# Nearest-neighbour upsampling on one core: rows owned in two blocks of 261 and 251 a partition, with new load and store sizes

## The chip, the core and the metric

The kernel runs on one core of one Trainium2 chip. The metric is the device time of one execution in microseconds, as the median of several executions. Besides the matrix engine, which does nothing here, the core has VectorE (DVE in the profile), ScalarE (ACT), GpSimd (POOL) and SyncE (SP). SP issues the DMA transfers of this kernel. The transfers are carried by 16 DMA engines that move data between HBM and the on-chip memory, which has 128 partitions.

## The reference: what is computed

The input `x` is a float32 array of 16 x 64 x 64 x 64 (batch, channel, row, column), 16.78 MB. Every pixel is repeated twice in each direction, which gives 16 x 64 x 128 x 128, or 67.11 MB:

```python
for i in range(new_h):
    for j in range(new_w):
        result[:, :, i, j] = x[:, :, i // scale_factor, j // scale_factor]
```

There is no arithmetic. The kernel reads every byte of the input once, copies it four times within the on-chip memory, and writes the copies.

## The kernel before, in words

All input rows of all images are numbered in one list of 65,536 rows of 64 floats (256 bytes). Partition p owns R = 512 rows that follow each other in memory: rows 512p to 512p + 511. One input row becomes two output rows of 128 floats, 1,024 bytes in all, which also follow each other in HBM, so that partition p's output is one piece of 512 KB. "A row" below always means an input row: 256 bytes to load, 1 KB a partition to store.

One on-chip tile, `mem`, holds everything. Its upper part, the view `xt`, takes the whole input (512 rows a partition). Below it are `FREE` = 79 rows' worth of output space, 79 KB a partition. Three loads bring in 8 rows, 248 rows and 256 rows a partition (`HEAD`, `cuts`, line 151). They are taken out of the kernel's body by `begin_before_barrier` and issued by SP as its first instructions.

The output is made in nine groups of 62, 32, 48, 64, 50, 64, 64, 64 and 64 rows (the list `rows`). For each group VectorE copies the rows into a buffer, with every element twice and every row twice (line 170, `expanded`); the first group takes two copies of 31 rows. Then SP stores the buffer with one transfer (line 171). There is one packet for each partition in each transfer, so each of the 16 DMA engines has eight packets of every transfer and works through its transfers in the order in which SP issues them.

Groups with an even number use the bottom of `mem`. Those with an odd number use a place that moves up: it ends where the input rows not yet expanded begin, and overwrites rows that have been expanded already. So a copy must wait until an earlier store has read its buffer: group 2 waits for store 0, group 3 for store 1, group 4 for store 2, and so on, always two groups back. Store n waits for copy n. Counting from 0, then, while store n - 1 moves, copy n has to run, so that store n is in the queue when store n - 1 ends. Group 4 is the one with 50 rows before the change.

`close_early` rewrites the end of the program so that the clearing of semaphores lies beside the last store; SP's last instruction waits for that store alone.

Of the kernel before, what the change touches and what calls it, by code (L numbers as in the profile page):

```python
# [1 line left out]

# [4 lines left out]

EARLY = 3  # L10


def begin_before_barrier(nc):

    blocks = nc.main_func.blocks
    main, body = blocks[0], blocks[1]
    sp = mybir.EngineType.SP
    loads = [i for i in body.instructions if i.engine == sp][:EARLY]  # L20
    for load in loads:
        assert isinstance(load, mybir.InstDMACopy), type(load)
        assert not (load.sync_info and load.sync_info.on_wait)
    names = [i.name for i in loads]
    body.instructions = [i for i in body.instructions if i.name not in names]
    kept = list(main.instructions)
    at = next(
        n
        for n, i in enumerate(kept)
        if i.engine == sp and isinstance(i, mybir.InstDrain)  # L30
    )
    kept[at:at] = loads
    main.instructions = kept


def close_early(nc):

    blocks = nc.main_func.blocks  # L40
    sp, pool = mybir.EngineType.SP, mybir.EngineType.Pool
    stores = [
        i
        for i in blocks[1].instructions
        if i.engine == sp and isinstance(i, mybir.InstDMACopy)
    ]
    last = stores[-1].sync_info.on_update[0].id

    end = list(blocks[-1].instructions)
    wait = end[0]  # L50
    assert wait.engine == sp and isinstance(wait, mybir.InstDrain)
    waits = list(wait.sync_info.on_wait)
    assert len({w.id for w in waits}) == len(waits) > 2
    assert all(w.wait_mode == "sem-ge-imm" for w in waits)

    mine = [i for i in end if i.engine == pool]
    kinds = [type(i).__name__ for i in mine]
    assert kinds == [
        "InstDrain",
        "InstEventSemaphore",  # L60
        "InstEventSemaphore",
        "InstDrain",
        "InstISA",
        "InstDrain",
        "InstEventSemaphore",
        "InstEventSemaphore",
    ], kinds
    d0, gather0, release0, d1, clear, d2, gather1, release1 = mine


    lo, hi = clear.ant_dict["range_first"], clear.ant_dict["range_last"]
    assert lo <= last <= hi and all(lo <= w.id <= hi for w in waits)
    clears = []
    for a, b in ((lo, last), (last + 1, hi + 1)):
        if a < b:
            clears.append(nc.gpsimd.sem_clear(range(a, b)).ins)

    landed = mybir.InstDrain(
        name=wait.name,
        engine=pool,  # L80
        debug=wait.debug,
        sync_info=mybir.SyncInfo(
            on_wait=[w for w in waits if w.id != last], on_update=[]
        ),
    )
    (w,) = [w for w in waits if w.id == last]
    final = mybir.InstEventSemaphore(
        name=clear.name,
        engine=sp,
        debug=wait.debug,  # L90
        sync_info=mybir.SyncInfo(
            on_wait=[w],
            on_update=[
                mybir.SyncUpdate(
                    sync_type=w.sync_type,
                    id=w.id,
                    ant_name=w.ant_name,
                    update_mode="sem-sub-imm",
                    update_value=w.wait_value,
                )  # L100
            ],
        ),
    )
    others = [i for i in end if i.engine != pool and i is not wait]
    blocks[-1].instructions = others + [
        d0, gather0, release0, gather1, release1, d1, landed, *clears, d2, final
    ]


@with_exitstack  # L110
def kernel(
    ctx: ExitStack,
    tc: tile.TileContext,
    x: bass.AP,
    scale_factor: int,
    out: bass.AP,
):
    nc = tc.nc
    nc.at_finalize(begin_before_barrier)
    nc.at_finalize(close_early)  # L120
    P = nc.NUM_PARTITIONS
    s = int(scale_factor)
    B, C, H, W = x.shape
    R = B * C * H // P
    fdt = x.dtype

    xp = x.rearrange("b c h w -> (b c h) w").rearrange("(p r) w -> p r w", p=P)
    op = out.rearrange("b c (h hd) w -> (b c h) (hd w)", hd=s).rearrange(  # L130
        "(p r) w -> p r w", p=P
    )

    rows = [62, 32, 48, 64, 50, 64, 64, 64, 64]
    GROW = s * s
    FREE = 79
    WF = FREE * GROW * W  # L140
    assert sum(rows) == R
    mem_pool = ctx.enter_context(tc.tile_pool(name="mem", bufs=1))
    mem = mem_pool.tile([P, WF + R * W], fdt, name="mem")
    xt = mem[:, WF:].rearrange("p (r w) -> p r w", r=R)

    HEAD = 8
    cuts = [0, HEAD, R // 2, R]
    for lo, hi in zip(cuts, cuts[1:]):  # L150
        nc.sync.dma_start(out=xt[:, lo:hi], in_=xp[:, lo:hi])  # L151

    def expanded(r0, r1):
        return (
            xt[:, r0:r1].unsqueeze(2).unsqueeze(4).to_broadcast([P, r1 - r0, s, W, s])
        )

    r0 = 0
    before = (0, 0)
    for n, k in enumerate(rows):  # L160
        size = k * GROW * W
        at = 0 if n % 2 == 0 else WF + r0 * W - size
        assert at >= before[1] or at + size <= before[0]
        before = (at, at + size)
        u = mem[:, at : at + size].rearrange(
            "p (k a w b) -> p k a w b", k=k, a=s, w=W
        )
        parts = [0, 31, k] if n == 0 else [0, k]
        for a, b in zip(parts, parts[1:]):
            nc.vector.tensor_copy(out=u[:, a:b], in_=expanded(r0 + a, r0 + b))  # L170
        nc.sync.dma_start(out=op[:, r0 : r0 + k, :], in_=u)
        r0 += k


# [1 line left out]
_INS = ['x', 'scale_factor']  # L176
_OUTS = [((16, 64, 128, 128), 'float32')]

_NUMBERS = {'scale_factor': 2}


# [26 lines left out]
```

## Time and profile before

| What | Value |
|---|---|
| Time, median of 3 runs (lowest to highest) | 197.09 us (197.07 to 197.12) |
| The profiled execution: its own time | 197.16 us |
| Its span, first to last instruction | 195.8 us |
| What lies around the span | 1.36 us |
| VectorE busy | 78.0 us (40% of the span), 10 copies |
| DMA packets, bytes | 1728, 83.89 MB |
| Share of the 16 DMA engines' span taken by packets | 99.2% |
| Mean rate over the span | 428 GB/s |

The profile gives the busy time of each engine, the busy share of the DMA engines in 40 slices, groups of instructions by form, and the chain of work that ended last. The trace behind it holds a start and a duration for every DMA packet too. An element of a shape is one float; "128x12800" is 128 partitions with 50 rows of 256 floats. A wait is named for what ended it: `DVE mem <- DMA out_dram<-mem` is VectorE waiting for a store.

### The profile page before, as it was taken

To read this page: it belongs to the slowest core of one execution; us is meant where nothing else is said; L and a number is where in the kernel's file an instruction comes from. 1 tells how busy PE (TensorE), PEld (TensorE's weight loads), DVE (VectorE), ACT (ScalarE), POOL (GpSimd) and SP (SyncE) were. 2 spreads that over 40 slices of the span, in tenths; PEclk is the share of its full clock that TensorE was granted. 3 is DMA by queue.
4 is the path that set the end of the run, shared out by engine and by line. 5 is a ranking of instruction groups with operands and counts; after the bars stand their busy time and mean duration, and the time that the engine had idled before them with its cause. 6 is when DMAs were issued, how large, how long until landed. Compare 5 with 4: busy or idle time off the path is not lost.

```text
span 195.8 us, 76 instructions
## 1 busy us (share of the span) xinstructions
DVE 78.0 (40%) x10; POOL 0.2 (0%) x4
## 2 busy tenths in 40 slices
DVE  0000599980007579085008907900890088000000
POOL 0000000000000000000000000000000000000000
DMA  9999999999999999899987989999999999999994
GB/s 456 415 428 415 428 428 428 428 415 415 415 415 428 428 482 482 375 469 495 469 384 345 502 348 455 442 469 482 469 442 428 428 428 442 428 428 428 428 428 214
DMA packets 1728, 83.89 MB, mean 428 GB/s; under 512 B 192, under 2 KB 192, under 8 KB 320
## 3 DMA queue, kind: packets, MB, share of 16 engines
q1 hardware_dynamic: 1728, 83.89, 99.2%
HBM read 16.78 MB, written 67.11 MB: 428 GB/s over the span
## 4 chain that ended last, share of the span: by engine, by line
DMA 60%; DVE 24%; SPq 0%; issue 0%; DVEq 0%
DMA out_dram<-mem 49%; DVE mem L170 24%; DMA mem<-in_x_dram 11%; SPq L151 0%; DVEq L170 0%
## 5 line engine op out<-in xcount | busy, mean ns | idle before, releaser
L170 DVE COPY mem<-mem 128x16384 f32<-128x16384 f32 (+4 forms) x10 | 78.0, 7812 | 87.8 <-DMA out_dram<-mem 65.8
L189 POOL MEMSET const-uint8-127<- 128x1 uint8 x1 | 0.1, 102 | 0.0
L189 POOL MEMSET const-bfloat16-1.0<- 128x1 bf16 x1 | 0.1, 101 | 0.0
L189 POOL MEMSET const-float32-0.0<- 128x1 f32 x1 | 0.1, 98 | 0.2 <-issue 0.2
L189 POOL MEMSET const-float32-1.0<- 128x1 f32 x1 | 0.1, 98 | 0.0
## 6 DMA issues: line engine op xcount, KB each, us to landing
mem<-in_x_dram SPq DMA_DIRECT2D x1, 7936.0 KB, 21.5
out_dram<-mem SPq DMA_DIRECT2D x1, 7936.0 KB, 21.2
out_dram<-mem SPq DMA_DIRECT2D x1, 6400.0 KB, 27.6
out_dram<-mem SPq DMA_DIRECT2D x1, 6144.0 KB, 17.5
out_dram<-mem SPq DMA_DIRECT2D x1, 4096.0 KB, 26.4
mem<-in_x_dram SPq DMA_DIRECT2D x1, 256.0 KB, 2.7
out_dram<-mem SPq DMA_DIRECT2D x5, 29.8
mem<-in_x_dram SPq DMA_DIRECT2D x1, 40.4
```

The costliest lines, as they stand in the source:

```text
L170: nc.vector.tensor_copy(out=u[:, a:b], in_=expanded(r0 + a, r0 + b))
L189: nc = _bacc.Bacc("TRN2", target_bir_lowering=False, num_devices=1)
```

## The change

The owner of a row changes. The first 128 x 261 rows of the list are block 0, in which partition p owns rows 261p to 261p + 260. The rest is block 1, in which partition p owns 251 rows. So a partition owns two pieces, and the distance in HBM between neighbouring partitions is 261 or 251 rows instead of 512. The loads are 256 and 5 rows of block 0 and the 251 rows of block 1; the small first load is gone. The groups are 62, 32, 52, 56 and 59 rows for block 0, and 64, 64, 64 and 59 rows for block 1. There are still three loads, nine stores and ten copies, and the buffers are placed by the same rule.

```diff
-    xp = x.rearrange("b c h w -> (b c h) w").rearrange("(p r) w -> p r w", p=P)
-    op = out.rearrange("b c (h hd) w -> (b c h) (hd w)", hd=s).rearrange(
-        "(p r) w -> p r w", p=P
-    )
-    rows = [62, 32, 48, 64, 50, 64, 64, 64, 64]
+    rows = [62, 32, 52, 56, 59, 64, 64, 64, 59]
+    SPLIT = 5
...
-    HEAD = 8
-    cuts = [0, HEAD, R // 2, R]
-    for lo, hi in zip(cuts, cuts[1:]):
-        nc.sync.dma_start(out=xt[:, lo:hi], in_=xp[:, lo:hi])
+    R0 = sum(rows[:SPLIT])
+    xf = x.rearrange("b c h w -> (b c h) w")
+    of = out.rearrange("b c (h hd) w -> (b c h) (hd w)", hd=s)
+    xp = [
+        xf[0 : P * R0].rearrange("(p r) w -> p r w", p=P),
+        xf[P * R0 : P * R].rearrange("(p r) w -> p r w", p=P),
+    ]
+    op = [
+        of[0 : P * R0].rearrange("(p r) w -> p r w", p=P),
+        of[P * R0 : P * R].rearrange("(p r) w -> p r w", p=P),
+    ]
+
+    HALF = R // 2
+    nc.sync.dma_start(out=xt[:, 0:HALF], in_=xp[0][:, 0:HALF])
+    nc.sync.dma_start(out=xt[:, HALF:R0], in_=xp[0][:, HALF:R0])
+    nc.sync.dma_start(out=xt[:, R0:R], in_=xp[1])
...
-        nc.sync.dma_start(out=op[:, r0 : r0 + k, :], in_=u)
+        blk = 0 if n < SPLIT else 1
+        f = r0 - blk * R0
+        nc.sync.dma_start(out=op[blk][:, f : f + k, :], in_=u)
```

## The prediction

> **What bounds the kernel now.** I read the page from the top: engines, DMA slices, queue.
>
> ```profile
> span 195.8 us, 76 instructions
> DVE 78.0 (40%) x10; POOL 0.2 (0%) x4
> ...
> DMA  9999999999999999899987989999999999999994
> ...
> q1 hardware_dynamic: 1728, 83.89, 99.2%
> ```
>
> The 16 DMA engines are busy from end to end; VectorE works 40% of the time. Only two things can move the time: what the DMA engines lose at the start, and any moment in which they have nothing queued. The rate itself is next, by windows (columns: window, its length, busy VectorE and POOL, clock, DMA share, GB/s); the first holds loads alone, the second stores alone.
>
> ```profile
> 22.00:38.00 16.00, 16.00 (x2) 0.00 (x0) 1.00 1.00 434
> 84.00:103.00 19.00, 6.83 (x1) 0.00 (x0) 1.00 0.98 427
> ```
>
> Loads and stores move at about one rate (a window counts packets where they begin, hence the small difference). The trace's packet records are steadier still: on every engine 64 KB packets follow each other every 2.414 us, loads or stores. Eight make a store of 64 rows, so a row costs 8 x 2.414 / 64 = 0.302 us.
>
> Then the groups by form, for the price of a copy (busy us, mean ns | idle before).
>
> ```profile
> L170 DVE COPY mem<-mem 128x16384 f32<-128x16384 f32 x5 | 43.5, 8694 | 43.3 <-DMA out_dram<-mem 43.3
> L170 DVE COPY mem<-mem 128x7936 f32<-128x7936 f32 x2 | 16.7, 8414 | 22.0 <-DMA mem<-in_x_dram 22.0
> L170 DVE COPY mem<-mem 128x12800 f32<-128x12800 f32 x1 | 6.8, 6827 | 5.7 <-DMA out_dram<-mem 5.7
> L170 DVE COPY mem<-mem 128x12288 f32<-128x12288 f32 x1 | 6.6, 6561 | 16.8 <-DMA out_dram<-mem 16.8
> L170 DVE COPY mem<-mem 128x8192 f32<-128x8192 f32 x1 | 4.4, 4427 | 0.0
> ```
>
> The second line is the odd one. Copies of 64, 50, 48 and 32 rows lie on one straight line: 0.521 ns an element and 160 ns fixed. The copy of 31 rows takes 8414 ns where that line gives 4.29 us: twice the price an element. It is the only form with an odd number of rows.
>
> Last, the chain of waits, in order of time, around group 4.
>
> ```profile
> 66.56 17.53 DMA out_dram<-mem
> 84.09 0.02 issue
> 84.12 6.84 DVE mem L170
> 90.96 0.02 issue
> 90.97 27.55 DMA out_dram<-mem
> ```
>
> Store 2 lands at 84.09; copy 4 (50 rows) runs until 90.96; store 4 is issued at 90.97 and sits behind store 3, whose last packets end, by the packet records, at 102.4 to 102.7 on 15 engines and 103.05 on the sixteenth. The copy is hidden with 11 us to spare.
>
> **The change, part by part.**
>
> *Bytes and transfers.* Three loads, nine stores, 83.89 MB and eight packets an engine in each transfer stay; SP issues as many DMAs in the same order, and POOL's closing work still lies beside the last store. Nothing.
>
> *The loads: the small head goes.* By the packet records the engines begin 1.00 to 1.33 us after SP starts the first issue. Their first 2 KB packets lose time: undisturbed, eight take 0.64 us, but the head ends at 1.92 to 2.38, so engines are 1.28 to 1.74 us late there. Then the first 62 KB packet of the second load loses another 0.06 to 0.38 us, and one engine also stands idle before it. That engine stays about 0.33 us behind the rest to the end: its last data ends at 195.44, and undisturbed work is 80 x 2.414 + 12 completions of 9 ns = 193.25, so it is 2.19 us late. Its lateness sets the time. With a first load of 256 rows the next packets wait in the queue from 2 us on, so I drop the second loss and keep the first: 1.74 late instead of 2.19, -0.45 us. Ends: 0, if large packets lose as much as head and successor together; -0.86, if an engine loses only its start at 1.33. The middle lies near the value taken. The five-row load lies in the full queue: eight small packets an engine, like the head's at 0.08 us each at most, in place of the head's. Nothing.
>
> *The row counts: two copies of 59 rows.* They are odd, like 31. At the 31-row price a copy of 59 rows takes 15104 x 1.042 + 150 ns = 15.88 us, at the even price 8.03. I take 15.88. The alternative reading, that the 31-row copies were slowed by loads running beside them, is spoken against by the 32-row copy, which shared its first 1.4 us with the loads and lies on the line.
>
> The Trainium skill, VectorE: DVE Perf Modes, section "Mode 2×_2P — use both read ports for one tensor", says the same from the other side: two elements a cycle need the outermost non-unit dimension even, or odd and equal in source and destination. Here the source's is the row count and the destination is one run, so by that rule 31 and 59 both fall to the slow rate; the trace agrees (8414 ns). Without the rule the sum below would lose its gap and end at -0.45.
>
> The last group's copy has cover. It begins when store 6 lands (157.16 before, five rows = 1.5 us later now), ends near 174.6, and store 7 occupies the engines until about 177: 2.3 us for a store to get going. Nothing.
>
> Group 4 has none. On the old clock: store 2 lands four rows later, 84.09 + 1.21 = 85.30. Copy 4 runs 85.33 to 101.21, store 4 is issued at 101.23. Store 3 now ends four rows earlier (202 rows against 206): 101.2 to 101.5 on 15 engines, 101.84 on the sixteenth. The queue runs dry 0.61 us after the issue at the latest. How long a store takes from its issue to its first packet with an empty queue, this trace doesn't show. Nearest row: the first load, 1.00 to 1.33 us to the first packet, up to 1.74 with the losses of its packets. From below: the issue instruction alone takes 0.33 us, and store 0, issued 1.4 us before the loads ended, left no gap, so a store needs at most 1.4. I take the last engine under way at 1.55, the middle of 1.33 and 1.74: a gap of 1.55 - 0.61 = +0.94 us, ends +0.05 (0.33 for the issue and 0.33 between engines) and +1.13. All engines have the same work left, so it stays to the end. Copies 5 and later begin from stores and keep 9 us.
>
> A sentence apart: the Trainium skill, DMA: Bandwidth & Descriptors, section "Latency and other measured facts", gives 600 ns to the first byte; by that the gap would be an estimated 0.4 us less and the sum about +0.1. The first load's 1.00 us disagrees.
>
> *The other even copies.* 52 and 56 rows take 7.1 and 7.6 us. Store 2 is then issued near 67.1, store 1 ends at 68.6 at the earliest: 1.5 us, where about 1.0 is needed. Nothing; if it failed, a few tenths.
>
> *The pitch* (261 and 251 rows between partitions): no row shows another pitch. Loads at 128 KB and stores at 512 KB between partitions have the same 2.414 us, so I take nothing; from above, the disturbed first packets at the start give up to 0.38 us a change of addresses.
>
> **Sum:** -0.45 + 0.94 = +0.49 us. The profiled execution is 197.16, the median 197.09; 197.09 + 0.49 = 197.6.
>
> **The rivals.**
>
> *A, not slower: the restart is hidden.* Place: the issue of store 4. If the last engine starts no later than 1.06 us after the issue, the gap is at most 0.45 and the head's gain pays for it; slower by 0.2% needs 1.45. For it: POOL, SP and the queue are warm by then, the first load came at the program's start. Against it: 1.00 to 1.33 is the only row. At 0.9 the time is 197.09 - 0.45 + 0.29 = 196.9; at 0.66 it is 196.7.
>
> *B, the gap without the gain.* The 64 KB packets lose at the start what head and second load lose now: 197.09 + 0.94 = 198.0. For it: the second loss sat in large packets on almost every engine.
>
> *C, the pitch disturbs.* Packets of neighbours no longer begin a power of two apart; with each new pitch (loads to stores, block 0 to 1, second load) all engines lose 0.06 to 0.38 us: 197.6 + 3 x 0.2 = 198.2. For it: the losses at the start are unexplained. Against: no loss at any later transfer boundary.
>
> *D, the pitch helps.* If the start's losses come from equal spacing, the engines begin at 1.33 and lose nothing: -0.86 + 0.94 = +0.1, 197.2; with the restart undisturbed too (1.33, gap 0.72), 197.0. The Trainium skill's DMA page, same section, has slow copies at row pitches of large powers of two (207 GB/s at 512 KiB), cured by padding; the stores here have that pitch and run at 427, so as a rate it is not borne out.
>
> *E, the 59-row copies are fast:* 197.09 - 0.45 = 196.6.
>
> **How the numbers follow.** Sum as forecast 0.45 (its own range 197.2 to 198.0; 0.33 of it slower, 0.12 within); A 0.18 (0.07 faster, 0.11 within); B 0.17, slower; C 0.10, slower; D 0.06, within; E 0.04, faster. Faster 0.11, same 0.29, slower 0.60. The bound of 0.2%, 0.39 us, is about what a measurement of this kernel can tell from no change. The range is 196.8 to 198.3: it takes in most of A, all of B and D and the lower half of C, and leaves out E and the ends of A and C, under 2 in 10.
>
> **What would show it.** In the profile after: a group 128x15104 near 15.9 us each, and in the DMA slices a dip near 101 us (slice 20 or 21). Store 4's first packets a microsecond and more after its issue; if they follow store 3's without a gap, the gap falls. The first copy starting near 21.5 instead of 21.99 is the head's gain; at 22.0 it is B. The 64 KB packets staying at 2.414 us refutes C. The prediction is wrong if 59 rows take 8 us, if the restart takes under 1.06 us, or if the packets slow down.

## The result and the profile after

The changed kernel takes 198.22 us (median of 6 runs, 198.07 to 198.34) against 197.06 for the kernel before (6 runs, 196.92 to 197.12). The ratio is 1.0059, with a 95% interval of 1.0046 to 1.0072: slower by 1.16 us. The profiled execution took 198.34 us, 1.18 more than that of before.

The page of the changed kernel, its totals:

```profile
span 197.0 us, 77 instructions
DVE 93.7 (48%) x10; POOL 0.2 (0%) x4
...
DMA  9999999999999998989989999999999999999996
...
q1 hardware_dynamic: 1728, 83.89, 98.9%
```

VectorE works 15.7 us more in as many copies. The DMA engines still look full everywhere: the loss hides in slices of 4.9 us. The dip that I had announced for slice 20 or 21 can't be told: counted from 0, slice 20 reads 8, as it did before the change. Where VectorE's time went is plain in the groups by form (busy us, mean ns | idle before):

```profile
L173 DVE COPY mem<-mem 128x15104 f32<-128x15104 f32 x2 | 31.8, 15886 | 18.7 <-DMA out_dram<-mem 18.7
L173 DVE COPY mem<-mem 128x16384 f32<-128x16384 f32 x3 | 26.1, 8694 | 21.4 <-DMA out_dram<-mem 21.4
L173 DVE COPY mem<-mem 128x14336 f32<-128x14336 f32 x1 | 7.6, 7626 | 2.6 <-DMA out_dram<-mem 2.6
L173 DVE COPY mem<-mem 128x13312 f32<-128x13312 f32 x1 | 7.1, 7094 | 16.9 <-DMA out_dram<-mem 16.9
```

A copy of 59 rows takes 15.89 us, almost twice one of 64 rows. The chain of waits around group 4:

```profile
67.50 18.24 DMA out_dram<-mem
85.74 0.03 issue
85.77 0.02 DVEq L173
85.79 0.04 issue
85.84 15.90 DVE mem L173
101.73 0.02 issue
101.75 19.25 DMA out_dram<-mem
```

Store 4 is issued at 101.75 and lands 19.25 us later. Undisturbed, 59 rows move in 17.8 us, so store 4 ran almost alone: nothing was left ahead of it. The DMA view of a window of 5 us shows the gap itself. It counts each packet where it begins, in 40 slices of 0.125 us:

```profile
GB/s 0 0 0 0 459 2294 918 1376 918 1376 0 0 0 0 0 0 0 0 0 0 0 0 0 0 0 0 0 0 3383 4350 0 0 0 0 0 0 0 0 0 0
```

The window is 99 to 104 us. The last packets of store 3 begin at 99.5 to 100.25, spread over 0.6 us. They take 2.11 us each, so the next ones were due at 101.7 to 102.3. They begin at 102.5 to 102.75, and nearly all together.

To add up the time I use the trace's packet records in one way throughout. The lateness of an engine is how far it lies behind a stream that had started at 0 and moved every packet undisturbed (2.414 us for 64 KB, others nearly in proportion, some 193.25 us in all; the choice of the total shifts all values alike by up to 0.03 us). The engine that is latest at the end sets the time. Its lateness, in us, in the two profiled executions and in some of those that follow:

| Lateness of the latest engine | before | after | even copies | head back | sizes, old pitch |
|---|---|---|---|---|---|
| after the loads | 2.16 | 2.56 | 2.19 | 2.25 | 2.27 |
| after store 3 | 2.17 | 2.66 | 2.20 | 2.26 | 2.28 |
| after store 4 | 2.17 | 3.14 | 2.20 | 2.70 | 2.80 |
| after store 8 | 2.18 | 3.38 | 2.21 | 2.92 | 3.05 |

In these two executions the changed kernel ends 1.20 us later than the kernel before: 0.40 from the loads, 0.09 in stores 0 to 3, 0.48 at the gap (packets of store 4 included), 0.24 in the stores after it less the 0.01 of before. Each column is one execution. Four of them lie within 0.12 us of their kernel's median time. That of the even copies does not: it took 197.16 us, the fastest of nine whose median is 197.63. It has the same loads as the changed kernel and ends them with a lateness of 2.19, not 2.56, so that a good part of the 0.40 can be scatter from one execution to the next.

### The profile page after: what moved, and what is told of

It reads as the page before. It is cut to its first block, busy times and chain, and to the rows that moved or that the text cites. A ratio compares the mean times of both kernels' runs of the same rounds, so it can differ in the third digit from the quotient of the medians.

```text
span 197.0 us, 77 instructions
## 1 busy us (share of the span) xinstructions
DVE 93.7 (48%) x10; POOL 0.2 (0%) x4
## 4 chain that ended last, share of the span: by engine, by line
DMA 56%; DVE 33%; issue 0%; DVEq 0%
DMA out_dram<-mem 45%; DVE mem L173 33%; DMA mem<-in_x_dram 11%; DVEq L173 0%
## 5 line engine op out<-in xcount | busy, mean ns | idle before, releaser
L173 DVE COPY mem<-mem 128x16384 f32<-128x16384 f32 (+5 forms) x10 | 93.7, 9383 | 81.9 <-DMA out_dram<-mem 59.6
```

## The experiments

Each was timed beside the kernel before on the same chip, but not all on one chip, so that kernels are best compared by their ratios. The kernel before had medians of 197.04 to 197.19 us here and scattered more than in the runs above (196.81 to 197.81), so that differences under about 0.2 us aren't settled.

| Kernel | Time, us | Ratio to before, 95% interval |
|---|---|---|
| changed, even copies | 197.63 | 1.0023 (1.0012 to 1.0034) |
| changed, head back | 197.85 | 1.0033 (1.0021 to 1.0045) |
| changed, both | 197.48 | 1.0015 (1.0006 to 1.0023) |
| before, no head | 197.42 | 1.0011 (1.0002 to 1.0020) |
| before, new sizes | 197.96 | 1.0041 (1.0028 to 1.0055) |
| before, new sizes, even copies | 197.04 | 0.9999 (0.9988 to 1.0011) |
| the same, loads cut at 261 | 197.44 | 1.0006 (0.9996 to 1.0016) |
| changed, 59 copied as 8 + 51 | 197.69 | 1.0032 (1.0021 to 1.0043) |
| before, head of 32 | 198.30 | 1.0060 (1.0045 to 1.0075) |
| before, store 0 early | 198.27 | 1.0051 (1.0038 to 1.0064) |
| before, head of 32, same wait | 197.50 | 1.0010 (0.9999 to 1.0020) |
| before, head of 4 | 197.38 | 1.0008 (0.9997 to 1.0019) |

**Even copies.** Only the copies of 59 rows are split.

```diff
         parts = [0, 31, k] if n == 0 else [0, k]
+        if k % 2:
+            parts = [0, k - 1, k]
```

> The changed kernel, with every copy of 59 rows made as 58 rows and 1 row; loads, stores and pitch as changed. Theory 1 (the 59-row copy empties the queue at store 4): two copies of 58 rows near 7.9 us, two of one row under 0.5 us, and no gap ahead of store 4. The gap in the changed kernel was 0.24 us on the engine that was last and about 0.95 on those that were first, so 0.25 to 0.45 us go: 197.8 to 197.95. Rival (the gap is all of the loss): 197.1. Rival (odd row counts don't set the rate of the copy): two copies in all cost as much as before and 198.2 stays.

The groups by form, and the window of 5 us from 99 to 104:

```profile
L175 DVE COPY mem<-mem 128x14848 f32<-128x14848 f32 x2 | 15.8, 7895 | 18.5 <-DMA out_dram<-mem 18.5
L175 DVE COPY mem<-mem 128x256 f32<-128x256 f32 x2 | 0.6, 286 | 0.0
```

```profile
GB/s 0 459 918 2753 1376 1376 459 0 0 0 0 0 0 0 0 0 0 0 483 967 2900 1450 1450 483 0 0 0 0 0 0 0 0 0 0 0 0 483 1450 2900 967
```

58 rows and one row take 8.2 us where 59 took 15.9. The packets of store 3, of store 4 and of store 4 again follow each other at even distances: the gap is gone. The time falls to 197.63, more than theory 1 gave to the gap (197.8 to 197.95). In this profile the stores after store 4 lose nothing more either: the latest engine stays at 2.20 to 2.21. But this is the execution of 197.16 us; what the median one lost in its stores isn't shown. That the 0.06 us a transfer behind the gap is a second cost of the copy is therefore only likely; the pair with new sizes and old pitch, below, speaks for it, and the run with 8 + 51 rows against it. Not all of the loss is gone, so the gap isn't all of it.

**Head back**, on the changed kernel:

```diff
-    HALF = R // 2
-    nc.sync.dma_start(out=xt[:, 0:HALF], in_=xp[0][:, 0:HALF])
-    nc.sync.dma_start(out=xt[:, HALF:R0], in_=xp[0][:, HALF:R0])
+    HEAD = 8
+    nc.sync.dma_start(out=xt[:, 0:HEAD], in_=xp[0][:, 0:HEAD])
+    nc.sync.dma_start(out=xt[:, HEAD:R0], in_=xp[0][:, HEAD:R0])
```

> The changed kernel, with loads of 8, 253 and 251 rows instead of 256, 5 and 251; copies of 59 rows whole. Theory 2 (without the small first load the engines lose more at the start): the loads' last data ends 0.4 us earlier (slowest engine 41.2 in the changed kernel, 40.8 before), the gap at store 4 stays, 197.8. Rival (the new pitch is to blame for the start): the start stays late, 198.2.

As theory 2 said: 197.85, loads ending with a lateness of 2.25 instead of 2.56, and the gap still there (2.26 to 2.70). **Both** edits together:

> The changed kernel with both: loads of 8, 253 and 251 rows, and 59 rows copied as 58 and 1. What is left of the change is the pitch (261 and 251 rows) and the sizes of the stores. Theories 1 and 2 together: 197.06 plus small losses of 0.01 to 0.05 us at each change of transfer that the changed kernel showed and the kernel before did not, some 0.2 us: 197.1 to 197.3. Rival (the pitch slows the start or the stores): 197.5 or more.

197.48, above the 197.1 to 197.3 of the two theories and just short of the rival's 197.5. In its profile (197.38) there is no gap and the loads end at a lateness of 2.11, but from store 3 on the latest engine slides to 2.42. Something of 0.1 to 0.2 us or more is left; the run with the loads cut at 261, below, comes back to it.

**No head, old pitch.** The kernel before with the changed kernel's loads:

```diff
-    HEAD = 8
-    cuts = [0, HEAD, R // 2, R]
+    cuts = [0, R // 2, 261, R]
```

> The kernel before, with loads of 256, 5 and 251 rows; one block, 512 rows a partition, groups as before. Theory 2 (the missing head costs the start): 197.06 + 0.4 = 197.45, slowest engine's loads ending near 41.2. Rival (the new pitch makes the start late, the head has no part): 197.06. Rival of the prediction (without the head the start is quicker by 0.45): 196.6.

197.42: the time goes the way of theory 2, and the prediction's gain of 0.45 is refuted. The first 64 KB packets begin 1.0 to 1.7 us after the issue, and the engines are 1.66 to 2.15 us late after that load. In the kernel before, the same 256 rows, as head and second load, leave them 1.48 to 2.16 late: large first packets lose as much as the head and its successor together. The interval of the ratio, 0.04 to 0.39 us, doesn't reach the 0.40 of the two profiles.

The sign that theory 2 gave for the trace did not come. The loads end at 40.83, as in the kernel before, and not near 41.2; the time in this profile (197.43) is lost in the stores, where one engine goes from 2.16 to 2.45. How late the loads end differs from execution to execution. By the lateness after the loads, the four profiles with loads of 256, 5 and 251 rows have 2.15, 2.19, 2.50 and 2.56, and the six with a head of 8 and no early store have 1.98 to 2.27. So the missing head costs some 0.2 us on average, and how is not shown.

**New sizes alone**, old pitch and loads:

```diff
-    rows = [62, 32, 48, 64, 50, 64, 64, 64, 64]
+    rows = [62, 32, 52, 56, 59, 64, 64, 64, 59]
```

> The kernel before with only the new list of groups (62, 32, 52, 56, 59, 64, 64, 64, 59); one block of 512 rows, loads of 8, 248 and 256. The 59-row copy is slow here too. Theory 1: a gap ahead of store 4 as in the changed kernel; with a first packet 0.83 to 0.98 us after the issue (measured there), 0.2 to 0.4 us on the last engine, then 0.06 us at each later transfer as in the two runs that had the gap: 197.5 to 197.7, the profile with a 128x15104 group near 15.89 us. Rival (the gap comes from the new pitch or loads): 197.1.

197.96, above the range of theory 1; the gap lies in the new sizes, whatever pitch and loads are. Store 4 is issued at 101.42 and the engines' first packets begin at 102.25 to 102.40: 0.83 to 0.98 us. In the changed kernel and with the head back it was 0.83 to 0.98 as well. This value is what the prediction lacked. The same sizes **with even copies** (the edit of the first run):

> The same with 59 rows copied as 58 and 1: new group sizes, old pitch, old loads, no slow copy. It differs from the run with head and even copies in the pitch and the cut of the loads alone, which stood 0.3 us above the kernel before. If the sizes of the stores are without effect: 197.1, and the 0.3 us belong to the pitch and the cut. If the sizes carry them: 197.4.

197.04, ratio 0.9999. The sizes themselves are free; the slow copies are worth 0.42% between these two, some 0.8 us. The two profiles (198.00 and 196.96, both near their medians) differ by 1.04: 0.51 at the gap, 0.25 in the stores behind it, and 0.29 in the loads, which these copies come too late to touch. In the two pairs with the new pitch, even copies gain 0.36% and 0.18%, 0.7 and 0.4 us.

**A shorter slow copy**, on the changed kernel:

```diff
+        if k % 2:
+            parts = [0, 8, k]
```

> The changed kernel with 59 rows copied as 8 and 51: 1.2 us at the fast rate and 13.75 at the slow one, 0.9 us less than the whole copy. Theory 1 with a restart of 0.83 to 0.98 us: the first packets of store 4 would come just when the engines run dry, gap 0 to 0.1 us, time as with 58 and 1, 197.6. With a restart of 1.55, the value of the prediction, a gap of 0.5 us or more is left on most engines, 198.0.

197.69, as theory 1 said. The chain around group 4:

```profile
85.68 14.90 DVE mem L175 x2
100.58 0.02 issue
100.59 19.76 DMA out_dram<-mem
```

Store 4 is issued at 100.59, and no engine waits: with 0.83 to 0.98 us to the first packet it could begin at 101.4 to 101.6, and the first engine is free at 101.67. One microsecond of a copy decides the gap. With 1.55 us most engines would have run dry still. The latest engine is 2.50 late after store 3 and 2.51 after store 4, but then loses some 0.05 us a transfer, to 2.70 after store 8: without any gap.

**The loads cut at 261**, with old pitch, new sizes and even copies: what is left of "both" without the pitch.

```diff
-    cuts = [0, HEAD, R // 2, R]
+    cuts = [0, HEAD, 261, R]
```

> One block of 512 rows, head of 8, the new groups with even copies, and the loads cut as 8, 253 and 251 rows: the run with head and even copies (197.48) with the old pitch alone put back. Pitch is what cost 0.3 to 0.4 us there: 197.05. The cut of the loads cost it: 197.4. In between, or with intervals that meet: scatter of the start, not settled.

197.44 in the median, but in two groups: four of twelve runs lie at 196.87 to 197.10, eight at 197.40 to 197.54. Its interval meets those of "both" and of the old cut. So the pitch is not shown to cost anything, nor cleared: a part of up to about 0.4 us stays open (the ratios differ by 0.0009, and their intervals allow 0.0022). The scatter has a pattern in the profiles. In some profiles two of the latest engines come within some tens of ns of each other, and from then on both, or the later one alone, lose some 0.06 us at each further transfer. It is no firm rule: in the run with even copies two engines 0.047 us apart lost nothing, nor did two 0.03 us apart in the next run. In this run's profile (197.50) the lateness creeps from 2.07 after the loads to 2.56 at the end, in that of 196.96 with the old cut it stays at 1.98 to 2.00.

**A head of 32 rows**, tried for a better start:

```diff
-    HEAD = 8
+    HEAD = 32
```

> The kernel before with a first load of 32 rows instead of 8 (loads of 32, 224 and 256). If the head's worth is that small packets lose less at the start, a larger head lies between 8 rows (197.1) and 256 rows (197.4): 197.2 to 197.3. If the loss is at the change from small to large packets while the queue is filling, a head that lasts longer saves some of it: 196.9. Both are near the scatter.

198.30, neither of the two. Nearly all of it is lost in one place: the eighth packet of the last load, which takes 3.19 to 3.92 us on the 16 engines instead of 2.42. The edit had moved more than the head. With 32 rows on chip the first copy of 31 rows needs no second load, so store 0 was issued at 30.38 instead of 38.77, and store 1 at 34.84. Two runs separate head and early store. **Store 0 early**, with the old head:

```diff
-        parts = [0, 31, k] if n == 0 else [0, k]
+        parts = [0, 30, k] if n == 0 else [0, k]
```

> The kernel before, with the first group's copies of 30 and 32 rows instead of 31 and 31: both even, 8.6 us instead of 16.8 in all, so that store 0 and store 1 are queued some 8 us before the loads end instead of 1.4 us. Theory E (a store queued behind a running load slows the end of the load, which the run with a head of 32 rows seemed to show with 0.8 to 1.5 us lost in the last load packet of every engine): 198.0 to 198.3. Rival (that loss belongs to the head of 32 rows): 197.05.

198.27: theory E. The window from 37 to 44 us, 40 slices of 0.175 us, for the kernel before and then for this one:

```profile
GB/s 0 0 0 0 1498 3745 374 0 374 0 0 0 0 0 0 0 0 0 1451 3628 363 363 0 0 0 0 0 0 0 0 0 1088 2902 1451 0 363 0 0 0 0
```

```profile
GB/s 0 0 0 0 0 1123 2621 2247 0 0 0 0 0 0 0 0 0 0 0 0 0 0 0 0 0 0 363 2902 1814 726 0 0 0 0 0 0 0 0 0 0
```

Before, the last load packets begin at 37.7 to 38.4 and the first of store 0 at 40.17, 2.4 us later. With store 0 queued at 30.21 and store 1 at 34.67, the distance is 3.6 to 3.9 us: every engine loses over a microsecond in its last load packet, ahead of its first store packet. **A head of 32 with the old wait** (first copies of 33 and 29 rows, both slow, both after the second load):

```diff
-    HEAD = 8
+    HEAD = 32
...
-        parts = [0, 31, k] if n == 0 else [0, k]
+        parts = [0, 33, k] if n == 0 else [0, k]
```

> The kernel before with a head of 32 rows, and first copies of 33 and 29 rows, which wait for the second load too and take 16.8 us in all: store 0 is issued as in the kernel before. Theory E: the loss of 1.2 us is gone, and the head of 32 lies between 8 rows (197.05) and 256 rows (197.4). Rival: 198.3 as with the early copy.

197.50: by the ratios 0.5%, 1.0 us, is gone with the early store, as theory E had it, and the last load packets take 2.42 us again; the head of 32 itself is no gain. In this profile (197.66) the loads end with a lateness of 2.24, and the latest engine slides to 2.68. Nor is **a head of 4 rows** (`HEAD = 4`):

> The kernel before with a head of 4 rows (1 KB packets): is the head's size at its best? Expected within 0.2 us of 197.05; above it if the engines run dry between head and second load, since four rows last 0.3 us.

197.38; its interval takes in the kernel before. No version tried beats the kernel before.

## Why the prediction was right, and where it was off

The direction, the place and the cause hold: 198.22 lies in the range of 196.8 to 198.3, near its upper end, and slower was the forecast. The move is 1.16 us where the sum gave 0.49, and it took luck that it fell within the range: two terms were wrong in opposite directions and one was missing. By the steps of the prediction:

- *The row counts.* 15.88 us a copy at the 31-row price: measured 15.886. That odd row counts set the rate is now shown by an edit (58 rows 7.90, 51 rows 13.75 us), and the reading that the loads slowed the 31-row copies falls, since 59 and 51 rows are as slow with no load under way. The Trainium skill, VectorE: DVE Perf Modes, section "Mode 2×_2P — use both read ports for one tensor", has this rule. The traces agree with it: 29, 31, 33, 51 and 59 rows are slow, all even counts are fast, and a single row, whose count is a unit dimension, takes 286 ns, the fast price. Rival E falls with it.
- *Group 4 has no cover.* Right, and the last group has, as worked out: store 8 followed store 7 without a gap.
- *The gap, +0.94.* Mis-sized, by the restart: 1.55 us was taken from the first load, 0.83 to 0.98 was measured. On the latest engine the gap cost 0.48, store 4's own packets included. A restart under 1.06 us was one of the prediction's own signs of being wrong, and it came: with 0.98 its sum would have been -0.45 + 0.37, no slower. That the kernel is slower all the same is owed to the next two terms. The Trainium skill, DMA: Bandwidth & Descriptors, section "Latency and other measured facts", gives about 600 ns to the first byte; the first engine needs 0.83 here, more than that and less than the 1.0 us of the first load.
- *What follows the gap.* Missing from the sum: "it stays to the end" was too little. After the gap all engines begin within 0.15 us of each other, and at each of the next four transfers they lose about 0.06 us, 0.24 in all. In the fastest execution with even copies, engines 0.55 us apart lost 2 ns a transfer. But other profiles without a gap lose as much in their stores (8 + 51 rows, no head, "both"), so that the gap is not shown to be the cause.
- *The loads, -0.45.* This step failed. It dropped the second loss and kept the first; in fact the large first packets lose as much as the head and its successor together, or more: 1.66 to 2.15 us late after 256 rows in the run without a head, up to 2.55 in the changed kernel, against 1.48 to 2.16 before. The first copy starts at 22.26, not near 21.5. In the profiled execution the term is +0.40, by the run without a head +0.2 (0.04 to 0.39); why the start scatters so stays open. That is rival B, whose condition was the end 0 of the term, and even that was too good. (The prediction's 80 x 2.414 + 12 x 0.009 is 193.23, not 193.25; the 2.19 moves by 0.02, and nothing hangs on it.) Rival B gave 198.0 with a gap of 0.94 and no loss at the start; the result has a smaller gap and a loss.
- *Rival A* (restart hidden) falls: it needed a start within 1.06 us after a gain that didn't come. *C and D*, the pitch: no disturbance at each change of address, and no cure of the start. All that can be held against the pitch is under some 0.4 us and not told from the scatter; that C's 198.2 is nearest to the result is chance, since the gap and the start, which have other causes, already give most of it.

So a gap twice too large and a start with the wrong sign partly made up for each other. In the profiled execution it is 0.48 + 0.23 + 0.40 + 0.09 in the place of 0.94 - 0.45.

## What to carry to other kernels

Where transfers bound a kernel, look at the one copy that has to fit under one transfer: here a list of sizes with a 59 in it turned 11 us of cover into none, because the row count was odd, and the cost showed only as a gap of under a microsecond in a DMA row that reads 8 and 9, as it did before. Keep the outer count of such copies even, or split one row off. And price a restart from an empty queue by a store that met an empty queue, not by the first transfer of the program.

## What I had not expected of the hardware

- With its first store queued 10 us before the loads end, and the second 5 us, the kernel takes 1.1 us more than with the first queued 1.4 us before (198.27 against 197.19, the kernel before on the same chip). The slow 31-row copies, which look like a fault of the kernel before, are what holds store 0 back; making them fast makes the kernel slower. Why the engines lose time there isn't shown; only that the loss follows the early stores and not the head.
- Engines that move nearly in step often lose time: 0.06 us a transfer after a common restart, in three profiles, and about as much in some profiles without one, where late engines lie close together. Two profiles with engines 0.03 and 0.047 us apart lost nothing, so this is a pattern and no rule. It would fit the two groups of times in the run with the loads cut at 261; when it sets in, and why, is not shown.
- From issue to first packet with an empty queue a store needs 0.83 us on the first engine and 0.98 on the last, three times alike; the first load of the program needs 1.0 to 1.33 in the kernel before, and up to 2.17 on one engine in the changed kernel.
